# A row gather on one core, with one more 512 KB write to HBM ahead of its gathers

## The chip, the core and the metric

The kernel runs on one core of a Trainium2 chip. The time is the device time of one execution in microseconds (us), less is better, and the comparison is made on the median of several runs. The core has five instruction streams (TensorE, VectorE, ScalarE, GpSimd and SyncE; in the profile PE, DVE, ACT, POOL and SP) and 16 DMA engines that move data between HBM and SBUF. This kernel computes nothing: all its work is DMA, and the instruction streams only issue transfers and wait for them.

## What is computed

For each of 32 batch entries, 128 rows of 1024 float32 numbers are picked out of 512 rows by a list of indices:

```python
x: (32, 512, 1024) float32;  indices: (32, 128), 0 to 511
for b in range(32):
    result[b] = x[b, indices[b]]        # 128 rows of 4 KB, 512 KB for each b
```

So 16.78 MB are read from HBM into SBUF and 16.78 MB are written back to HBM.

## The kernel before

The kernel works one batch entry at a time, and everything is unrolled: there are 32 steps. Each step has two transfers of 512 KB.

- The *gather* (L35 in the profile): GpSimd starts an indirect DMA that reads 128 rows of `x` at the places that a column of indices names, and puts one row into each of the 128 SBUF partitions of the tile `block{b}`. Its transfers run on the queue that the profile calls q0.
- The *store* (L41): the tile is written to the output as one contiguous piece of 512 KB. Even steps issue it from SyncE, odd steps from ScalarE. SyncE's transfers run on the queue q1, ScalarE's on q10. This can be seen from the small packets of the index loads, whose numbers differ between the two.

Every step has its own tile, so no gather waits for a tile to come free. A store waits for the gather that fills its tile. There are eight semaphore slots for GpSimd's transfers, so that the gather of step k waits until the gather of step k-8 has landed.

Ahead of the 32 steps the indices are loaded (L27), turned so that one batch entry is one column over the 128 partitions. They come in four pieces: column 0 from SyncE, columns 1 to 3 from ScalarE, columns 4 to 11 from SyncE, and columns 12 to 31 from ScalarE. Each packet of these loads holds only 8 bytes, so they have many packets and few bytes. The gather of step 0 waits for the first piece alone, and so on.

The order of issue on each engine is the order of the code. The tile framework adds the semaphores and, at the end (L67), a wait for all that is under way.

Of the kernel before, what the change touches and what calls it, by code (L numbers as in the profile page):

```python
# [5 lines left out]


@with_exitstack
def kernel(ctx, tc, x, indices, out):

    nc = tc.nc
    B, S, D = x.shape
    N = indices.shape[1]
    const = ctx.enter_context(tc.tile_pool(name="const", bufs=1))
    rows = ctx.enter_context(tc.tile_pool(name="rows", bufs=1))  # L20

    by_row = indices.rearrange("b n -> n b")
    at = []
    cuts = [(0, 1, nc.sync), (1, 4, nc.scalar), (4, 12, nc.sync), (12, B, nc.scalar)]
    for c, (lo, hi, eng) in enumerate(cuts):
        part = const.tile([N, hi - lo], indices.dtype, name=f"idx{c}")
        eng.dma_start(out=part[:], in_=by_row[:, lo:hi])  # L27
        words = part[:].bitcast(mybir.dt.int32)
        at += [words[:, 2 * k:2 * k + 1] for k in range(hi - lo)]

    xf = x.flatten_outer_dims()
    of = out.flatten_outer_dims()
    for b in range(B):
        block = rows.tile([N, D], x.dtype, name=f"block{b}")
        nc.gpsimd.indirect_dma_start(  # L35
            out=block[:], out_offset=None,
            in_=xf[:], in_offset=bass.IndirectOffsetOnAxis(ap=at[b], axis=0),
            element_offset=b * S * D,
        )
        eng = nc.sync if b % 2 == 0 else nc.scalar  # L40
        eng.dma_start(out=of[b * N:(b + 1) * N], in_=block[:])  # L41


# [1 line left out]
_INS = ['x', 'indices']  # L45
_OUTS = [((32, 128, 1024), 'float32')]


def kernel(**inputs):
    import numpy as _np  # L50
    import concourse.bacc as _bacc
    import concourse.tile as _tile
    from concourse import mybir as _mybir
    from concourse.bass_utils import run_bass_kernel_spmd as _run

    nc = _bacc.Bacc("TRN2", target_bir_lowering=False, num_devices=1)  # L56
    arrays, args = {}, []
    for name in _INS:
        a = _np.ascontiguousarray(inputs[name])
        if a.dtype.kind in "iu":  # L60
            a = a.astype(_np.int64)
        arrays[f"in_{name}_dram"] = a
        args.append(nc.dram_tensor(f"in_{name}_dram", a.shape, _mybir.dt.from_np(a.dtype), kind="ExternalInput").ap())
    for i, (shape, dtype) in enumerate(_OUTS):
        dt = _mybir.dt.from_np(_np.dtype(dtype))
        args.append(nc.dram_tensor(f"out_{i}_dram", shape, dt, kind="ExternalOutput").ap())
    with _tile.TileContext(nc) as tc:  # L67
        kernel(tc, *args)
    r = _run(nc, [arrays], core_ids=[0])
    got = tuple(r.results[0][f"out_{i}_dram"] for i in range(len(_OUTS)))  # L70
    return got[0]
```

## Time and profile before

| | |
|---|---|
| median of 8 runs | 91.11 us (91.06 to 91.37) |
| the profiled execution, its own time | 91.31 us |
| its span, first to last instruction | 89.5 us |
| time outside the span in that execution | 1.8 us |
| POOL busy | 30.3 us in 36 instructions |
| DMA over the whole span | 33.59 MB, mean 375 GB/s |
| DVE, PE | no instruction |

The profile counts as busy only the work of the engines, not the issue of a DMA on SyncE or ScalarE. What a DMA does is read from the table of the DMA queues (packets, bytes, and the share of the 16 engines' time), and from tables of stretches of the span, which give for each stretch the mean busy share of the 16 DMA engines ("DMA share") and what they moved ("GB/s"). A byte that goes from HBM to SBUF, or back, is counted once. A packet is put down to the stretch in which it starts, so that a share can come out a little over 1. "Landing" is the time from the issue of a transfer until its semaphore shows all of it as done.

### The profile page before, as it was taken

How to read it: one execution, taken by the hardware profiler on the slowest of the kernel's cores; microseconds unless marked ns; L12 is line 12 of the kernel's file. 1: busy time of each engine (PE TensorE's matmuls, PEld its weight loads, DVE VectorE, ACT ScalarE, POOL GpSimd, SP SyncE). 2: the span in 40 equal slices, each digit the busy share in tenths (PEclk: the TensorE clock that was granted, in tenths of full speed). 3: DMA queues.
4: the chain of work that ended last, by engine and by line, in shares of the span. 5: the costliest groups of instructions: out<-in, count | busy, mean ns of one | idle time of the engine just before them, and what ended most of it. 6: DMA issues, size and time to landing. Idle time of an engine off the chain costs nothing.

```text
span 89.5 us, 146 instructions
## 1 busy us (share of the span) xinstructions
POOL 30.3 (34%) x36
## 2 busy tenths in 40 slices
POOL 0677777644443342244444332234440000000000
DMA  1989799999999999999999999999999999999990
GB/s 2 13 253 309 194 357 426 417 417 425 417 417 425 417 419 423 419 419 423 419 417 425 417 421 423 415 423 421 415 426 417 417 425 419 417 425 417 417 403 35
DMA packets 13377, 33.59 MB, mean 375 GB/s; under 512 B 5185, under 2 KB 5185, under 8 KB 13377
## 3 DMA queue, kind: packets, MB, share of 16 engines
q0 software_dynamic: 4608, 16.78, 47.5%
q10 hardware_dynamic: 5280, 8.41, 24.7%
q1 hardware_dynamic: 3488, 8.40, 23.6%
q14 instruction: 1, 0.00, 0.0%
HBM read 16.81 MB, written 16.78 MB: 375 GB/s over the span
## 4 chain that ended last, share of the span: by engine, by line
DMA 60%; POOL 7%; issue 5%; POOLq 1%
DMA block<-in_x_dram,idx 58%; POOL block L35 7%; DMA idx<-in_indices_dram 2%; POOLq L67 1%
## 5 line engine op out<-in xcount | busy, mean ns | idle before, releaser
L35 POOL DMA_INDIRECT block<-in_x_dram,idx x32 | 30.1, 940 | 35.8 <-DMA block<-in_x_dram,idx 30.2
L56 POOL MEMSET const-float32-0.0<- 128x1 f32 x1 | 0.1, 98 | 0.2 <-issue 0.2
L56 POOL MEMSET const-uint8-127<- 128x1 uint8 x1 | 0.1, 118 | 0.0
L56 POOL MEMSET const-bfloat16-1.0<- 128x1 bf16 x1 | 0.1, 112 | 0.0
L56 POOL MEMSET const-float32-1.0<- 128x1 f32 x1 | 0.1, 104 | 0.0
## 6 DMA issues: line engine op xcount, KB each, us to landing
out_dram<-block SPq DMA_DIRECT2D x16, 512.0 KB, 6.6
out_dram<-block ACTq DMA_DIRECT2D x16, 512.0 KB, 6.6
block<-in_x_dram,idx POOLq DMA_INDIRECT x32, 19.6
idx<-in_indices_dram ACTq DMA_DIRECT2D x1, 20.0 KB, 3.9
idx<-in_indices_dram ACTq DMA_DIRECT2D x1, 3.0 KB, 1.9
idx<-in_indices_dram SPq DMA_DIRECT2D x1, 1.0 KB, 1.8
idx<-in_indices_dram SPq DMA_DIRECT2D x1, 8.0 KB, 3.3
```

The source lines that it names most:

```text
L35: nc.gpsimd.indirect_dma_start(out=block[:], out_offset=None, in_=xf[:], in_offset=bass.IndirectOffsetOnAxis(ap=at[b], axis=0), element_of ...
L56: nc = _bacc.Bacc("TRN2", target_bir_lowering=False, num_devices=1)
L67: with _tile.TileContext(nc) as tc:
```

## The change

Between the loads of the indices and the 32 steps, a tile `fill` of 128 partitions by 1024 float32 is made and set to zero by VectorE, and SyncE issues one DMA that writes it, 512 KB in 128 rows of 4 KB, to an HBM buffer `scratch` of the kernel's own. Nothing reads this buffer. In SyncE's order the new transfer stands behind the two index loads and ahead of the first store. Nothing else is altered.

```diff
         eng.dma_start(out=part[:], in_=by_row[:, lo:hi])
         words = part[:].bitcast(mybir.dt.int32)
         at += [words[:, 2 * k:2 * k + 1] for k in range(hi - lo)]
+
+
+    scratch = nc.dram_tensor("scratch", (N, 1024), mybir.dt.float32, kind="Internal").ap()
+    fill = const.tile([N, 1024], mybir.dt.float32, name="fill")
+    nc.vector.memset(fill[:], 0.0)
+    nc.sync.dma_start(out=scratch, in_=fill[:])
 
     xf = x.flatten_outer_dims()
     of = out.flatten_outer_dims()
```

## The prediction, made before the changed kernel had run

> **What bounds the kernel now.** I read the page first, its row of 40 slices above all, then a table of stretches cut at the places where that row changes, then a finer table of the first 14 us, then the queues in two of those stretches, and last the timeline of the issues. The page's DMA rows:
>
> ```profile
> DMA  1989799999999999999999999999999999999990
> GB/s 2 13 253 309 194 357 426 417 417 425 417 417 425 417 419 423 419 419 423 419 417 425 417 421 423 415 423 421 415 426 417 417 425 419 417 425 417 417 403 35
> ```
>
> From the seventh slice to the last but one the 16 DMA engines are full, at 415 to 426 GB/s. Only the first six slices (13.4 us) are below that. The stretches say it in five rows; the columns are the stretch, its length, POOL's busy time, the TensorE clock (of no account here), the DMA share and GB/s:
>
> ```profile
> 0.50:4.50 4.00, 1.43 (x2) 1.00 0.57 8
> 4.50:12.00 7.50, 5.67 (x7) 1.00 0.83 257
> 12.00:18.00 6.00, 4.27 (x5) 1.00 1.02 416
> 18.00:84.50 66.50, 18.72 (x20) 1.00 1.03 420
> 84.50:88.50 4.00, 0.00 (x0) 1.00 0.74 302
> ```
>
> The reader is to see three times. Up to 4.5 us only index packets move. From 4.5 to 12 us there is work, but 257 GB/s instead of about 417: 1.93 MB moved in 7.5 us, where 3.13 MB could have; 1.20 MB, or 2.9 us of full DMA, are lost. From 12 us on there is always more queued than the engines can move, so every byte not moved by then comes off the end at 420 GB/s. The chain of waits names gathers ("DMA block<-in_x_dram,idx 58.1%"), but those are waits for the eighth gather back, that is, for a full DMA. So the question is what the new transfer does to the bytes moved by 12 us. The finer table:
>
> ```profile
> 3.50:4.00 0.50, 0.34 (x1) 1.00 1.51 21
> 4.00:4.50 0.50, 0.36 (x1) 1.00 0.40 6
> 4.50:5.00 0.50, 0.50 (x1) 1.00 1.31 156
> 5.00:5.50 0.50, 0.20 (x2) 1.00 0.37 106
> 5.50:6.00 0.50, 0.50 (x1) 1.00 1.00 410
> 6.00:6.50 0.50, 0.32 (x1) 1.00 0.85 344
> ...
> 9.50:10.00 0.50, 0.50 (x1) 1.00 0.73 197
> 10.00:10.50 0.50, 0.20 (x2) 1.00 0.71 164
> 10.50:11.00 0.50, 0.50 (x1) 1.00 0.68 131
> 11.00:11.50 0.50, 0.28 (x1) 1.00 0.63 213
> ```
>
> There are two weak places: 4.5 to 5.5 us, the first packets of the first gather, and 9.5 to 11.5 us. The queues from 9.5 to 12 us:
>
> ```profile
> q0 software_dynamic: 109, 0.40, 60.2%
> q1 hardware_dynamic: 30, 0.12, 11.9%
> ```
>
> Gathers (q0) and the first store (q1) together moved 0.52 MB in 2.5 us, 1.25 us less than full speed. Yet the store was issued at 7.29 us, and POOL had issued gathers at 2.77, 4.14, 5.39, 6.63, 7.87 and 9.11:
>
> ```profile
> 7.29 0.35 SPq L41 DMA_DIRECT2D out_dram<-block  x1
> 7.87 0.93 POOL L35 DMA_INDIRECT block<-in_x_dram,idx  x1 [0.30 <-issue]
> ```
>
> So work was issued that the DMA engines were not yet doing. The profile does not show why.
>
> **The change part by part.**
>
> *The memset.* VectorE has no other instruction, so the memset begins when the streams start, about 0.7 us (the first index loads go out at 0.74). The trace has no DVE row. The nearest is POOL's memset of 128x1, 98 to 118 ns, which gives the fixed part only, and so a floor of 0.1 us. The Trainium skill, "VectorE: DVE Perf Modes", section "Zero memsets can be issued as uint32 (trn2)", counts one cycle per element; at the 0.96 GHz of "Trainium Kernel Development and Optimization", "NeuronCore Architecture", 1024 elements are an estimated 1.07 us. I take 1.1 us, end at about 1.8. It is hidden: nothing but the new DMA waits for it. If it were twice as long, the new DMA would go out at 2.9, still before the first gather has data moving.
>
> *The new wait and issue on SyncE.* SyncE issues its two index loads at 0.74 and ends at 1.60 (0.86 us for both). Then it waits for the memset, and issues for about 0.35 us (as a store does, 332 to 355 ns), ending at about 2.2. Behind it on SyncE stands only the first store at 7.29. Cover 5 us, cost nothing. ScalarE and POOL are not held.
>
> *The transfer.* 128 packets of 4 KB are 0.524 MB, or 1.26 us of all 16 engines at 417 GB/s. When does it run? An index load issued at 0.74 has its first packets near 2.0, so 1.2 us of latency: 3.1 to 3.4. It stands in q1 behind the index columns 4 to 11, whose packets last to about 3.8 (q1 has 357 small packets between 3 and 4.5 us and q10 2427, most of them after q1's). So the transfer starts between 3.4 and 4.7 and would be over between 4.9 and 6 us. The last index piece (q10) is mixed with it and comes later by up to 1.3 us; it is needed by the gather of step 12, issued at 18.31, while it lands at about 5.1. Cost nothing, cover over 10 us.
>
> *The first gather beside it.* Here is the cost. A rule of the Trainium skill speaks against the change: "DMA: Bandwidth & Descriptors", "Issuing engines are not separate DMA queues", says that transfers from all issuing engines run on the same 16 DMA engines and interleave. By that rule alone the sum is plus 1.26 us, as the kernel is DMA-bound from start to end: 92.4. The trace's rows weaken it: between 4.5 and 12 us the share is 0.83, so 0.17 x 7.5 = 1.28 us of all 16 engines is idle (by chance almost the size of the transfer), and a further 1.6 us is lost in packets that take longer than at full speed. The other end is plus 0: all of it fits in. Between them: the first gather lands at 7.2 us, with 0.73 MB moved by q0 from 4.5 to 7.3. Of the transfer, 0.3 to 1.3 us falls beside it, and its own slow first microsecond takes some of that. I take the first gather 0.5 to 0.8 us later. The next two gathers are issued by then and wait in q0, and at full speed instead of 80% q0 makes up for it by 9.5 us: 128 new packets and some 300 of gathers need 4.3 us from 4.5, so 8.8. What is late next is the first store, issued when the first gather has landed: 7.9 instead of 7.29. Its packets are then 0.6 us late in the weak stretch from 10 to 12.5 us, where they are about half of what moves at its end (46% of the engines against 48.6% from 12 to 14). 0.6 us at 0.55 to 0.6 of the engines, the rest idle or gathers, is 0.3 to 0.4 us of full DMA. Sum: plus 0.4 us.
>
> *The end.* SyncE's final wait has one more semaphore, landed 80 us before: nothing. The semaphore slots of the stores move round by one; the transfer eight back is long done: nothing.
>
> The changes are sums against the profiled execution (91.31, span 89.5): 91.7 and a span of 89.9. The median before is 0.20 lower, so the forecast for the median is 91.11 + 0.4 = 91.5.
>
> **The rivals.**
>
> *Fully paid (92.4).* For it: q0 has work issued from 4 us on, so any packet ahead of it delays it. Against: the idle 1.28 us. Needs the weak stretch to shift with the first gather.
>
> *Absorbed (91.1).* For it: if gathers from 4.5 to 12 us are held by how fast POOL's descriptors come, 257 GB/s is POOL's rate and not the DMA's, and the new transfer takes idle time. Also, if it starts at 3.4, most of it is over before 4.8. Against: POOL issues one every 1.24 us, which is 423 GB/s.
>
> *Faster (90.2).* One mechanism: the weak stretch at 9.5 to 11.5 us is what the first 512 KB write to HBM costs on cold engines. The first store's first packets come 2.9 us after its issue (7.29 to 10.2), and gathers thin out just then. If the new write pays this at 3.5 to 6 us, when there is little to delay, the 1.25 us of 9.5 to 12 come back, less the 0.4 above: about minus 0.9. For it: at no later step is there such a hole. Against: the store issued at 85.02 landed in an unloaded queue within 3.4 us, but one issued in the full stretch takes 6.6 to landing, so 2.9 us to the first packet is no sign of a cold path. It decides against my forecast once over 0.6 us of the hole is gone.
>
> **How the numbers follow.** Partly absorbed, plus 0.2 to 0.9, likeliest 0.4: 0.40. Fully paid, 0.9 to 1.4: 0.13. Absorbed, within 0.2% (0.18 us, about what a measurement of this kernel can tell from no change): 0.17. Faster, minus 0.2 to 1.6: 0.30. So slower 0.53, same 0.17, faster 0.30. The likeliest case alone is 91.3 to 92.0. The range of 90.2 to 92.4 leaves out the lower half of the faster case and the tail of the fully paid one, about 2 in 10.
>
> **What would show it.** Right: a DVE memset of about 1.1 us, a fill on q1 between 3.4 and 6 us, the first store issued near 7.9, the row of 12 to 18 us still at 416 GB/s, and the weak stretch at 9.5 to 11.5 still there, shifted a little. Fully paid: the same curve, 1.2 us later throughout. Absorbed: the first store near 7.3 and more than 2.4 MB moved from 4.5 to 12. Faster: 350 GB/s or more from 9.5 to 12 us. The forecast is wrong in its mechanism if the hole goes or widens by more than half a microsecond.

## The result: 0.6% faster, and the profile after

The changed kernel takes 90.58 us (median of 11 runs), the kernel before 91.12 us (median of 32 runs taken beside it). The ratio is 0.994, with a 95% interval of 0.9926 to 0.9953. So half a microsecond is gained, where 0.4 us of loss was forecast. The profiled execution took 90.59 us, its span is 88.8 us; before, these were 91.31 and 89.5. The ratios compare fast executions alone: one that is more than 1.5% above the fastest of its kernel is left out, which touches the write from ScalarE (2 of 12), the copy from SBUF to SBUF (3 of 10) and the read with the exchanged index queues (1 of 6).

The first view is the page of the changed kernel, its rows of 40 slices of the span (2.2 us each): the DMA share in tenths, and GB/s.

```profile
DMA  1998999999999999999999999999999999999990
GB/s 2 122 312 332 373 389 371 419 426 415 417 423 422 421 413 423 422 423 415 423 419 423 419 417 423 422 421 413 424 419 424 415 421 421 426 415 417 421 413 31
```

The fifth slice had 194 GB/s before and has 373 now; the dip is gone. The plateau at about 420 GB/s is the same. The second view is the table of stretches of the changed kernel. Its columns are the stretch, its length, VectorE's and POOL's busy time, the TensorE clock, the DMA share and GB/s:

```profile
0.50:4.50 4.00, 0.91 (x1) 1.42 (x2) 1.00 0.59 74
4.50:12.00 7.50, 0.00 (x0) 5.67 (x7) 1.00 1.01 345
12.00:18.00 6.00, 0.00 (x0) 4.47 (x6) 1.00 1.02 394
18.00:84.50 66.50, 0.00 (x0) 18.54 (x20) 1.00 1.03 420
84.50:88.50 4.00, 0.00 (x0) 0.00 (x0) 1.00 0.58 235
```

From 18 to 84.5 us both kernels move 420 GB/s, so in these two executions the difference lies ahead of that. Up to 12 us the kernel before moved 8 x 4.0 + 257 x 7.5 = 1.96 MB (GB/s times us, in kB). The changed one moved 74 x 4.0 + 345 x 7.5 = 2.88 MB, of which 0.52 MB is the new write, so 2.36 MB of useful data. That is 0.40 MB more, worth 0.95 us at 420 GB/s. From 12 to 18 us it gives 22 GB/s back (394 against 416), 0.13 MB or 0.31 us. The rest is 0.64 us; the span is 0.7 us shorter. The new write was more than paid for by the same 12 us in which it ran.

That this sum comes out so well is partly luck. The kernel with the memset alone (the first experiment below) has the same span as the kernel before, 89.5 us. By 18 us its profiled execution had moved 0.21 MB more, worth 0.5 us, and it lost that at its end. Two of its stretches, one in the weak place and one at the end:

```profile
9.50:12.00 2.50, 0.00 (x0) 1.89 (x3) 1.00 0.85 277
...
85.50:86.00 0.50, 0.00 (x0) 0.00 (x0) 1.00 0.33 131
```

So a sum over stretches of one execution can be off by about as much as the gain, and the weak place of the kernel before (208 GB/s) is in this execution less deep (277) at no gain in time.

The finer table of the changed kernel shows where the bytes are gained:

```profile
4.00:4.50 0.50, 0.00 (x0) 0.35 (x1) 1.00 1.09 403
...
10.00:10.50 0.50, 0.00 (x0) 0.20 (x2) 1.00 0.95 360
10.50:11.00 0.50, 0.00 (x0) 0.50 (x1) 1.00 0.94 352
```

From 4 to 4.5 us, where 6 GB/s were read before, the new write now moves. From 10 to 11 us, where 164 and 131 GB/s were read before, the engines are now busy, and the queues of the changed kernel from 9.5 to 12 us say with what (packets, MB, share of the 16 engines):

```profile
q0 software_dynamic: 200, 0.72, 74.5%
q1 hardware_dynamic: 61, 0.24, 23.5%
```

Gathers (q0) moved 0.72 MB instead of 0.40, and the first store (q1) 0.24 instead of 0.12. POOL did not issue them sooner: up to 12 us its gathers start at the same times to 0.01 us as before. The timeline of the changed kernel gives the new steps and the first store (start, duration; the last row merges three stores, of which the first starts at 8.02):

```profile
1.02 0.91 DVE L34 MEMSET fill<- 128x1024 f32 x1 [1.02 <-PEq L62]
1.96 0.34 SPq L35 DMA_DIRECT2D scratch<-fill  x1
...
8.02 8.15 SPq L47 DMA_DIRECT2D out_dram<-block  x3
```

The first store goes out at 8.02 us instead of 7.29. So the first gather is 0.73 us later, and yet more has been moved by 12 us.

Up to 9.5 us the two kernels are level. Here is q0 from 4.5 to 9.5 us, first before and then after:

```profile
q0 software_dynamic: 379, 1.41, 89.1%
...
q0 software_dynamic: 367, 1.37, 78.3%
```

They have then moved 2.7 and 2.6 gathers of 0.52 MB each, and in both POOL has begun to issue the sixth. So from 9.5 us on the changed kernel has no more gathers waiting than the kernel before; they run faster. The packet records of the two traces say what is different: from 9.5 to 12 us the middle packet of a gather takes 0.16 us in both, but before, 22 of 97 of them took more than 0.3 us, and after, 5 of 175. The hole is made of single packets that stand for long, and of engines that are idle meanwhile.

### The profile page after: what moved, and what is told of

The parts are those of the page before. It is cut to its first block, busy times and chain, and to the rows that moved or that the text cites. A ratio compares the mean times of both kernels' runs of the same rounds, so it can differ in the third digit from the quotient of the medians.

```text
span 88.8 us, 149 instructions
## 1 busy us (share of the span) xinstructions
DVE 0.9 (1%) x1; POOL 30.3 (34%) x36
## 4 chain that ended last, share of the span: by engine, by line
DMA 60%; POOL 8%; issue 5%; POOLq 1%
DMA block<-in_x_dram,idx 58%; POOL block L41 8%; DMA idx<-in_indices_dram 2%; POOLq L73 1%
## 5 line engine op out<-in xcount | busy, mean ns | idle before, releaser
L34 DVE MEMSET fill<- 128x1024 f32 x1 | 0.9, 912 | 1.0 <-PEq L62 1.0
```

The source lines that it names most:

```text
L34: nc.vector.memset(fill[:], 0.0)
```

## The experiments

Every kernel below was timed in five rounds beside the kernel before on the same chip; the ratio is to that kernel. Diffs are against the kernel before unless they say otherwise. A range in brackets is the 95% interval of the ratio. The theories that the expectations name are these:

- **W**: the first bulk write to HBM is slow once, and the new write pays for it early. This is the forecast's rival "faster".
- **B**: the transfer holds the DMA engines at the start, while POOL goes on issuing. More gathers are then queued behind the one that runs, and the engines no longer run dry.
- **R**: a bulk read of HBM ahead of the gathers makes the path warm for them.
- **Q**: the transfer has to be on SyncE's queue.
- **I**: the gain comes from the long index piece (20 columns, 2560 packets of 8 bytes) being pushed to beside the first gather.

### The memset alone

```diff
+    fill = const.tile([N, 1024], mybir.dt.float32, name="fill")
+    nc.vector.memset(fill[:], 0.0)
```

> The 0.9 us memset on VectorE is kept, the 512 KB write is left out. Every theory that puts the gain in the transfer (the first write to HBM being slow once; the first gather starting later, with more gathers queued behind it) expects no change: ratio 0.998 to 1.002, about 91.1 us, first store issued near 7.3 us, 9.5 to 12 us at about 208 GB/s. A ratio near 0.994 would put the gain in the memset or the new wait on SyncE.

Measured: 91.2 us, ratio 1.0006 (0.9985 to 1.0026). The memset brings and costs nothing; the gain is the transfer's.

### A write of 64 KB

```diff
-    nc.sync.dma_start(out=scratch, in_=fill[:])          # of the changed kernel
+    nc.sync.dma_start(out=scratch[:, 0:128], in_=fill[:, 0:128])
```

> The write is cut to 64 KB: 128 packets of 512 B instead of 4 KB. Theory W (the first write to HBM is slow once and the new write pays for it early): the gain stays and its cost shrinks from 1.26 us of DMA to about 0.2, so a ratio of 0.982 to 0.992 (89.5 to 90.4 us), and 350 GB/s or more from 9.5 to 12 us. Theory B (the first gathers start 0.7 us later, so that more gathers are queued when they run and the DMA engines do not run dry): so short a transfer delays nothing, the hole at 9.5 to 12 us comes back (about 208 GB/s), ratio 0.998 to 1.003.

Measured: 91.23 us, ratio 1.0006 (0.9988 to 1.0024). 64 KB were written to HBM ahead of the gathers, and nothing was gained. Its stretches of 7 to 9.5 and 9.5 to 12 us remain weak:

```profile
7.00:9.50 2.50, 0.00 (x0) 1.89 (x3) 1.00 0.86 262
9.50:12.00 2.50, 0.00 (x0) 1.89 (x3) 1.00 0.88 269
```

This speaks against W; that a cold cost needs 512 KB to be paid is left to the next run.

### A read in place of the write

```diff
-    nc.sync.dma_start(out=scratch, in_=fill[:])          # of the changed kernel
+    nc.sync.dma_start(out=fill[:], in_=x.flatten_outer_dims()[0:N])
```

> The transfer has the same size, place, queue and time but runs the other way: it reads 512 KB of x (contiguous rows) into the tile, and writes nothing to HBM. Theory W: nothing is paid early, the hole at 9.5 to 12 us stays, and the transfer costs 0.3 to 1.3 us: ratio 1.003 to 1.014. Theory B: it delays the first gather as the write does, so it gains as the write does: ratio 0.992 to 0.996, 350 GB/s or more from 9.5 to 12 us.

Measured: 89.81 us, ratio 0.9891 (0.9845 to 0.9937). It writes nothing to HBM ahead of the gathers and gains 1.1% where the write gains 0.6%. W has fallen. The engines are full in both stretches:

```profile
7.00:9.50 2.50, 0.00 (x0) 1.89 (x3) 1.00 1.04 413
9.50:12.00 2.50, 0.00 (x0) 1.89 (x3) 1.00 1.02 410
```

### The write from ScalarE

```diff
-    nc.sync.dma_start(out=scratch, in_=fill[:])          # of the changed kernel
+    nc.scalar.dma_start(out=scratch, in_=fill[:])
```

> The same 512 KB write issued from ScalarE (q10) instead of SyncE (q1). If what is paid early belongs to SyncE's queue, the first store, which is on q1, meets it again: hole back, ratio 1.000 to 1.014. Theory W for HBM writes whatever the queue, and theory B: ratio 0.992 to 0.996; the write stands behind the 20 index columns on q10, so the first gather may be up to 0.5 us later than in the changed kernel.

Measured: 91.64 us, ratio 1.0067 (1.0033 to 1.0101). Theory B as it stood then had expected a gain, so this was a miss for it (0.992 to 0.996 was expected), and the question of the queue was open.

### From SBUF to SBUF

```diff
-    nc.sync.dma_start(out=scratch, in_=fill[:])          # of the changed kernel
+    copy = const.tile([N, 1024], mybir.dt.float32, name="copy")
+    nc.sync.dma_start(out=copy[:], in_=fill[:])
```

> The 512 KB go from the zeroed tile to a second SBUF tile, same place and queue (q1): the DMA engines are held as long, and HBM is not touched. Theory B (what counts is that the engines are held at the start while POOL issues gathers ahead): gain as with the write or more, ratio 0.988 to 0.995, and 9.5 to 12 us at 350 GB/s or more. Theory R (what counts is that HBM is read in bulk before the first gather, so that the gathers meet a warm read path): no gain, ratio 1.002 to 1.010, 9.5 to 12 us near 210 to 290 GB/s.

Measured: 90.9 us, ratio 0.9934 (0.9902 to 0.9966). A transfer that does not touch HBM gains. It is the least sure of the gains: over all ten executions the median is only 0.25% below that of the kernel before. Its stretch of 9.5 to 12 us has 311 GB/s, short of the 350 that B expected. R is not needed, and W is out once more.

### The read from ScalarE, and half and an eighth of the read

```diff
+    nc.scalar.dma_start(out=fill[:], in_=x.flatten_outer_dims()[0:N])            # read on ScalarE
+    nc.sync.dma_start(out=fill[0:64], in_=x.flatten_outer_dims()[0:64])          # 256 KB
+    nc.sync.dma_start(out=fill[:, 0:128], in_=x.flatten_outer_dims()[0:N, 0:128])  # 64 KB
```

> The 512 KB read of the last round, issued from ScalarE (q10) instead of SyncE (q1). Theory Q (the transfer has to run on SyncE's queue, where it also holds back the last index piece; on q10 it comes behind that piece): no gain, ratio 1.002 to 1.010, as the write on q10. Theory R and theory B: ratio 0.985 to 0.994, as the read on q1 (0.9891).

> The read on SyncE with half the bytes: 64 rows of 4 KB. It costs 0.63 us of all DMA engines instead of 1.26. Theory R: the warm path stays, and 0.6 us more is gained than with 512 KB: ratio 0.980 to 0.986. Theory B: the gathers start about 0.6 us earlier than with 512 KB, fewer are queued, and a part of the hole comes back: ratio 0.990 to 0.998.

> The read on SyncE with 128 packets of 512 B, 64 KB in all. It holds the engines for about 0.2 us. Theory R: nearly the whole lost time comes back, ratio 0.975 to 0.986. Theory B: nothing is delayed and nothing gained, ratio 0.998 to 1.002, as with the 64 KB write.

Measured: the read on ScalarE 91.28 us, ratio 1.0025 (1.0011 to 1.004); 256 KB 90.44 us, ratio 0.9911 (0.9889 to 0.9933); 64 KB 91.12 us, ratio 0.9997 (0.9984 to 1.001). The 64 KB read gains nothing, so R has fallen; half the bytes gain about as much as all of them. On ScalarE's queue the read loses as the write did; R and B had both expected a gain of 0.6 to 1.5%, so this is a second miss for B. The profile of the read on ScalarE shows when it ran, here q10 from 3 to 4.5 us and from 4.5 to 6 us:

```profile
q10 hardware_dynamic: 2455, 0.06, 105.7%
...
q10 hardware_dynamic: 106, 0.43, 92.7%
```

It stands behind the long index piece, so its bulk begins shortly ahead of 4.5 us, when the first gather would begin (156 GB/s from 4.5 to 5 us in the kernel before). In the changed kernel, on SyncE, the transfer stands behind the short index piece: it moved 403 GB/s from 4 to 4.5 us, and a part of the small packets was pushed back instead.

This run speaks against B in the form given above. The transfer holds the engines longer than in the changed kernel (the first store goes out at 8.76 us), and by 9.5 us q0 has moved only 1.04 MB, so more gathers are waiting than in any kernel that gained. Yet its stretches of 7 to 9.5 and 9.5 to 12 us stay weak, with the engines full:

```profile
7.00:9.50 2.50, 0.00 (x0) 1.89 (x3) 1.00 0.98 288
9.50:12.00 2.50, 0.00 (x0) 1.89 (x3) 1.00 1.01 323
```

From 9.5 to 12 us 24 of 197 gather packets took over 0.3 us, where the read on SyncE has none.

### The long index piece moved

```diff
+        if c == 3:
+            nc.vector.memset(hold[:], 0.0)      # 128x2560 float32, or 128x7680
+            nc.vector.memset(part[:].bitcast(mybir.dt.float32), 0.0)
         eng.dma_start(out=part[:], in_=by_row[:, lo:hi])
```

> No extra transfer. The last index piece (20 columns, q10) is held back by a memset on VectorE of about 2.3 us, so that ScalarE issues it near 3.4 us and its small packets move beside the first gather, from about 4.6 to 6.2 us, as they do in the kernels that gained. Theory I (the gain comes from the last index piece moving beside the first gather and not before it): gain without the cost of the transfer, ratio 0.980 to 0.993. Theory B (the gain comes from the gathers queuing up while the engines are held): the first gather starts as before, ratio 0.997 to 1.005.

> The control for the next run: no extra transfer, the last index piece held back by a memset of about 6.9 us, issued near 8 us, its packets from about 9 to 12 us. Theory B: no change in the gathers up to 9 us, then up to 1 us of DMA time more in the weak stretch: ratio 0.998 to 1.008. Theory I: no gain either, as the piece is now beside the third gather: 0.995 to 1.008.

> The 512 KB read on SyncE (which gave 0.9891) with the last index piece held back to about 9 us as in the run before it. Theory B: the gain stays, 0.986 to 0.994. Theory I: with the small packets away from the first gather the gain goes, and the read costs its 0.3 to 1.3 us: 1.003 to 1.014.

Measured: held back by the shorter memset 90.85 us, ratio 0.9951 (0.9932 to 0.997); by the longer one 92.5 us, ratio 1.0148 (1.0124 to 1.0172); the longer one with the read 92.3 us, ratio 1.0107 (1.0086 to 1.0128).

The first two lie outside both ranges; the third lies in the range of I (1.003 to 1.014), but for another reason. The last two can't decide what they were made for. The late index piece, 20 KB in small packets, took 22.1 us to land beside full queues (3.9 us before), and POOL waited 15.2 us for it before the gather of step 12. That is a new wait, not the effect in question. The first one gains 0.5% with no extra transfer and no delay of the first gather, more than B and less than I expected. It is ambiguous: the small packets came later than meant and hold the engines from 6.5 to 8 us, and after that its stretch of 9.5 to 12 us has 352 GB/s.

The read of 256 KB settles I. These are its queues from 4.5 to 6 us, all of them:

```profile
q0 software_dynamic: 39, 0.16, 56.9%
q1 hardware_dynamic: 44, 0.11, 37.9%
```

No packet of q10 is there: the long index piece was over before the first gather moved data, as in the kernel before, and 0.9% was gained. So the gain does not need the small packets beside the first gather, and I has fallen.

### The two index queues exchanged

The pieces of 8 and 20 columns are exchanged between ScalarE and SyncE, and the transfer goes on ScalarE, so that it again stands ahead of the long piece and not behind it.

```diff
-    cuts = [(0, 1, nc.sync), (1, 4, nc.scalar), (4, 12, nc.sync), (12, B, nc.scalar)]
+    cuts = [(0, 1, nc.sync), (1, 4, nc.scalar), (4, 12, nc.scalar), (12, B, nc.sync)]
...
+    nc.scalar.dma_start(out=fill[:], in_=x.flatten_outer_dims()[0:N])            # read
+    nc.scalar.dma_start(out=scratch, in_=fill[:])                                # or write
+    nc.scalar.dma_start(out=fill[0:64], in_=x.flatten_outer_dims()[0:64])        # or 256 KB
```

> The 512 KB read on ScalarE (q10), with the two long index pieces exchanged: columns 4 to 11 on ScalarE, columns 12 to 31 on SyncE. So the read again stands behind the shorter piece and ahead of or beside the longer one, as in the run that gave 0.9891, with the two queues exchanged. If the place against the long index piece counts and not the queue: ratio 0.985 to 0.994. If the transfer has to be on SyncE's queue, which carries the first store: 1.000 to 1.008, as the read on ScalarE without the exchange (1.0025).

> The exchange of the two long index pieces between SyncE and ScalarE, with no extra transfer: the control for the read that gave 0.9833 with it. If that gain is the transfer's, the exchange alone gives 0.997 to 1.003; if it is the exchange's, 0.983 to 0.992.

> The 512 KB write on ScalarE with the index pieces exchanged, as the read that gave 0.9833. Theory B: what counts is that the transfer lies ahead of the long index piece, not its queue: 0.985 to 0.996, where the write on ScalarE behind that piece gave 1.0067. If writes differ from reads, 1.000 or more.

> Half of the read, 64 rows, on ScalarE with the index pieces exchanged, tried as the fastest version. Theory B: it holds the engines for 0.6 us less, so fewer gathers queue up: the cost falls by 0.6 us and a part of the gain goes, 0.984 to 0.993.

Measured: the read 89.89 us, ratio 0.9833 (0.9801 to 0.9865); the exchange alone 91.1 us, ratio 1.0 (0.9982 to 1.0017); the write 90.71 us, ratio 0.9944 (0.9929 to 0.996); the read of 256 KB 90.49 us, ratio 0.9902 (0.9865 to 0.994). So Q has fallen: what counts is the place against the long index piece. It is not that the bytes move earlier there. The write stands on q10 in both cases; from 3 to 4.5 and from 4.5 to 6 us, q10 first with the write behind the long piece (1.0067), then with the exchange (0.9944):

```profile
q10 hardware_dynamic: 2373, 0.11, 103.9%
q10 hardware_dynamic: 99, 0.40, 97.3%
...
q10 hardware_dynamic: 918, 0.04, 38.3%
q10 hardware_dynamic: 257, 0.49, 84.0%
```

With the exchange less of the write has moved by 4.5 us, and the first store goes out later (9.04 us against 8.44), and yet it gains. Why the place counts was not found. The read with the exchange has the lowest ratio of all, and its interval overlaps with that of the read on SyncE. The read of 256 KB was tried as the fastest version and is not.

### POOL slowed down

```diff
     for b in range(B):
         block = rows.tile([N, D], x.dtype, name=f"block{b}")
+        if 1 <= b <= 6:
+            nc.gpsimd.memset(pad[:], 0.0)       # 128x256 float32, kept in this place
         nc.gpsimd.indirect_dma_start(
```

> No extra transfer; between the first seven gathers POOL does a memset of 128x256 (0.2 to 0.4 us), so that fewer gathers are queued while the first ones run. The first gather is not delayed. Theory B (the DMA engines run below full speed at the start because too few gathers are queued behind the one that runs): the weak stretch gets deeper, under 280 GB/s from 4.5 to 9.5 us, ratio 1.004 to 1.020. If the gathers are slow there for another reason than POOL's lead (a cold path, a slow engine), POOL's lead is not what is short, and nothing changes: 0.998 to 1.002.

Measured: 91.77 us, ratio 1.0061 (1.0042 to 1.008). A memset took 0.33 us, and the seventh gather was issued at 11.51 us instead of 10.36. The sign is as B says and the size is at the low end of its range (1.004 to 1.020). The place is not: its profiled execution (91.32 us, less than its median) moves more, not less, than the kernel before from 4.5 to 12 us (322 GB/s against 257), and less after that. Here are its rows of 9.5 to 12 and 12 to 18 us (POOL, clock, share, GB/s):

```profile
9.50:12.00 2.50, 2.17 (x5) 1.00 1.00 349
12.00:18.00 6.00, 4.47 (x6) 1.00 0.95 350
```

The kernel before had 208 and 416 there. So in this execution the hole stands later; it is not the same one deepened. One profiled execution, as fast as that of the kernel before, does not settle how these holes form, nor where the 0.6% goes.

### Small packets in place of the bulk transfer, and the bulk transfer with a slower POOL

```diff
+    spare = const.tile([N, 20], indices.dtype, name="spare")
+    nc.sync.dma_start(out=spare[:], in_=by_row[:, 12:B])      # the first of the two
```

The second kernel has the 512 KB read on SyncE and the six memsets on POOL.

> No bulk transfer: the long index piece is loaded a second time, by SyncE into a tile that nothing reads, 2560 packets of 8 bytes (20 KB), which hold the DMA engines for about 1.1 us as the first such load does. Theory B (the engines are held while POOL gets ahead, whatever holds them): ratio 0.988 to 0.997, first store near 8 us, no hole at 9.5 to 12 us. If 4 KB packets are needed, of whatever direction, because bulk packets alter how the later gathers run: no gain, 1.000 to 1.010.

> The 512 KB read on SyncE (0.9891) together with POOL's six memsets (alone 1.0061). Theory B: POOL's lead is what the read gives, and the memsets take most of it away again: the gathers no longer run at full speed from 7 to 12 us, and the two together are 0.998 to 1.010. If the read makes the packets themselves faster and POOL's lead is of no account for that, the two effects add up or the memsets cost nothing beside it: 0.989 to 0.996.

Measured: the index piece loaded twice 90.49 us, ratio 0.9921 (0.9892 to 0.9951); the read with POOL's memsets 91.19 us, ratio 1.0007 (0.9983 to 1.0031). First, 20 KB that nobody needs, in packets of 8 bytes, gain about as much as 512 KB in packets of 4 KB, so neither bulk packets nor many bytes are needed. In its profile the small packets on q1 and q10 take most of the engines' time from 3 to 6 us (packets, MB, share):

```profile
q1 hardware_dynamic: 2951, 0.02, 55.5%
q10 hardware_dynamic: 2471, 0.02, 46.3%
```

From 7 us on the engines run at full speed, as its table of stretches says (POOL, clock, share, GB/s):

```profile
7.00:9.50 2.50, 1.89 (x3) 1.00 1.01 398
9.50:12.00 2.50, 1.89 (x3) 1.00 1.03 401
```

Second, the read that alone gave 0.9891 gives nothing when POOL issues its gathers 0.19 us further apart, and the weak stretch is back (the read with the memsets):

```profile
9.50:12.00 2.50, 0.00 (x0) 2.17 (x5) 1.00 0.89 269
```

The memsets alone cost 0.61%, beside the read they cost 1.16% (1.0007 - 0.9891). If the two simply added up, the ratio would be 0.9952; the measured one is 0.0055 above that, and the three intervals together allow about as much (0.0046, 0.0019 and 0.0024, added as squares 0.0055). So that a slower POOL takes away the read's gain, beyond its own cost, is likely but not clear of the noise.

## Why the prediction was wrong

**What held.** The engines are full from 18 us on at 420 GB/s in both kernels, and what is moved ahead of that makes most of the difference. The memset was put at 1.1 us and took 0.91; it began at 1.02 and not at 0.7, and it is hidden, as the kernel with the memset alone shows. (The longer memsets of the index runs, 2560 and 7680 elements in 2.19 and 6.46 us, give 0.83 ns for each further element, where the text's estimate has 1.04.) The issue on SyncE came at 1.96 us and took 0.34. The transfer ran at the time given: 0.27 MB moved on q1 from 3 to 4.5 us and 0.25 from 4.5 to 6. The first store was forecast at 7.9 us and went out at 8.02. The delay of the first gather was thus right in size (0.73 us, forecast 0.5 to 0.8). So was the remark that the transfer and the long index piece mix, and also that q0 would make up for the delay by 9.5 us: it had moved 1.37 MB against 1.41.

**Two readings that were too strong.** The last slice but one of the kernel before has 403 GB/s, so the plateau does not reach to it at 415 to 426. And not every byte that is left at 12 us comes off the end at 420 GB/s: the execution with the memset alone fell to 131 GB/s from 85.5 to 86 us.

**The step that failed** is "The first gather beside it", and in it the sentence that a late first store loses 0.3 to 0.4 us because its packets are late in the weak stretch. This took the hole at 9.5 to 12 us as fixed in place, with a loss to be added to it. It is not fixed: from 208 GB/s it went to 383, which is 175 x 2.5 = 0.44 MB or 1.04 us at 420 GB/s. Against the execution with the memset alone (277) it is 0.27 MB or 0.63 us. Either in place of the 0.4 of loss turns the sign. The text's own mark for "faster", 350 GB/s or more from 9.5 to 12 us, was met. The text had even seen that issued work was not being done, and that the profile did not show why; then it costed the delay as if that did not matter. That the measured time still lies within 90.2 to 92.4 is due to the share that the range gave to the rival "faster", and not to this step.

**The argument that misled** stands under the rival "absorbed": POOL issues a gather every 1.24 us, which is 423 GB/s, so POOL can't be short. That is a comparison of mean rates, and it was used as if it showed that POOL's pace is of no account. Making POOL 0.19 us slower for six gathers costs 0.6%, so its pace does count. That POOL's lead is what the change improves does not follow: at 9.5 us the lead is the same before and after.

**The rule of the Trainium skill** that all transfers share the same 16 engines, "DMA: Bandwidth & Descriptors", section "Issuing engines are not separate DMA queues", gave plus 1.26 us by itself. The trace agrees on the sharing: in the changed kernel q0, q1 and q10 move side by side from 4.5 to 6 us (36.5, 41.7 and 40.2% of the 16 engines). The sum does not hold: on SyncE the 512 KB gain 0.6 to 1.1%, and on ScalarE behind the long index piece the loss is 0.2% for the read and 0.7% for the write, which is 0.2 and 0.6 us.

**The rivals.** "Faster" had the sign and, at minus 0.9 us where 0.54 was measured, the right order of size; that was luck, as its mechanism, a cold first write, is refuted by three kernels: a read, an SBUF copy and an index load that write nothing to HBM ahead of the gathers and gain 0.7 to 1.1%. "Absorbed" named POOL's pace as what holds the gathers, which the slowed POOL supports in part, but drew from it that the write would merely be free.

**What is shown, and what stays open.** The gain is the transfer's: not the memset's, not that of a write, of HBM, of bulk packets or of one queue. It needs more than 64 KB in 128 packets, and a place ahead of the long index piece. Of the gather packets that start from 9.5 to 12 us, 13 to 24 take more than 0.3 us in the kernels that gain nothing or lose, and at most 4 in the reads on SyncE, the read of 256 KB with the exchange and the second index load, which gain 0.8 to 1.1%. (Where less is gained the count does not tell: the changed kernel has 5, the SBUF copy 18, the write with the exchange 13.) Why these packets stand, and why work ahead of the first gather removes them, was not found. Of theory B it is seen that in every kernel that gained by a transfer the first gather's first packet comes later, at 4.96 to 5.80 us instead of 4.55. That more gathers are then queued, and that this is why the engines stay full, is not seen. The transfers on ScalarE behind the long piece, where that packet comes at 6.0 us, speak against it, and the slower POOL alone, whose profile shows the hole later, doesn't decide. Nor was it found why the read gains more than the write: 0.9891 against 0.994 on SyncE, 0.9833 against 0.9944 with the exchange.

## What to carry to other kernels

Where a profile has a start-up below full speed with work already issued, the time of something that is put ahead of it can't be priced by its bytes: here transfers that nobody needs gained 0.6 to 1.7% in one place and lost 0.2 to 0.7% in another. Such a thing is to be measured in several places. Try it first with a load that is needed anyway, moved there, before one that is not: issuing the last index piece some 2.4 us later gave 0.5% with no added byte, and issuing it some 8.7 us later lost 1.5%. And where a stretch of the trace is weak for a reason that the profile doesn't show, a delay ahead of it can go either way; such a step needs a wide range of both signs, not a loss.

## What the hardware showed that was not expected

- Packets of 8 bytes hold the DMA engines out of proportion. In the kernel before, 2427 of them (19 KB) took 90.7% of the 16 engines from 3 to 4.5 us, or 1.4 us of all of them (the 1.1 us in the expectation above is too low); 512 KB at 420 GB/s take 1.25 us. The second load of this piece has about the same effect on the kernel's start as 512 KB in 128 packets.
- The same 20 KB load landed in 3.9 us at the start and needed 22.1 us when it was issued beside full queues.
- The same 512 KB write gives 0.994 on SyncE behind 8 index columns, 0.9944 on ScalarE behind 8, and 1.0067 on ScalarE behind 20.
- Gathers can run below full speed with several issued, and the loss is in few packets: the middle one takes 0.16 us from 9.5 to 12 us in the kernel before and in the changed one, while 22 of 97 took over 0.3 us before and 5 of 175 after.
